# An encoder trunk's instruction planner: two DMA queues that share the rings, a margin behind each landing, and rotary queries written as whole rows

## The chip, the core and the metric

One core of a Trainium2 chip runs the whole program as one launch. TensorE (PE) multiplies, and its weight loads (PEld) overlap the multiplications; VectorE (DVE) and ScalarE (ACT) do elementwise work; GpSimd (POOL) and SyncE (SP) issue DMAs here and compute next to nothing. The metric is the device time of one execution in microseconds (us), as a median of several.

## The reference, cut to what matters

```python
for l in range(2):                                   # x: (1, 512, 1024) float32
    h = rmsnorm(x, g_mix[l])
    y_a = differential_attention(rope(h @ Wq), rope(h @ Wk), h @ Wv)   # 4 heads, two softmaxes each
    y_b = dilated_attention(...)                     # 3 (window, dilation) groups, 4 heads each
    c_q, c_kv = rmsnorm(h @ Wcq), rmsnorm(h @ Wckv)  # MLA: 768 and 256 wide
    qh = (c_q @ w_uq).reshape(S, 8, 64 + 32)         # 8 heads: 64 plain and 32 rotary columns
    q = concat(qh[..., :64], rope(qh[..., 64:]))     # the rotary part is the one rewritten
    y_c = softmax(q @ k.T * 96 ** -0.5) @ v
    x = x + (sum(sigmoid(gate_i) * y_i) ) @ w_out[l]
    x = x + square(relu(rmsnorm(x, g_mlp[l]) @ w_up[l])) @ w_down[l]
return rmsnorm(x, g_final)
```

## The kernel before, in words

Activations lie transposed: 128 features on the partitions, 512 tokens along the row. Every product is taken in three passes of float32r: weights and activations are split into a high and a low half, and `mm3` issues high x high, high x low and low x high. So each block of weights goes through the same steps: a DMA into a buffer `raw`, an ACT copy `w<-raw` (high half), a DVE subtraction `w<-raw,w` (low half), and then some 24 matmuls of 512 columns. Most weight loads are issued by POOL; those of the rotary query/key units (`qk_unit`, labels du0 to du3, bs0, bs1, bo00 to bo11) and of `w_uq` (labels rq and mq0 to mq3) are issued by SP, together with all small transfers.

The engines' work is first recorded and then planned. `trunk` calls engine objects whose methods only append an `Op` to a `Plan`; `record` finds its predecessors and `cost` its assumed duration. `Plan.schedule` then plays the program through, event by event: each engine takes, of its operations that are ready, the one with the lowest key, if its buffers can be had (42 slots of 1024 words, at most 6 of them `raw`). `emit` writes the operations out in the order of their planned starts, one order over all engines. On the chip only each engine's own order and the semaphores count; the planned times exist nowhere. An engine takes its instructions strictly in that order, so an ACT copy whose load is late holds back every ACT instruction behind it.

Of a DMA the plan assumes a transfer time `lat` on the 16 engines and an extra time `more`; one number `pipe` says when the transfers entered so far are through, whichever queue issued them. When a DMA is finished in the plan, its readers on compute engines become ready `dslack` (100 ns) later:

```python
if op.eng in dmaq and ops[s].eng not in dmaq:
    f += o["dslack"]
```

The program of a layer: `ckv` and `cq` (MLA inputs), `KV`, then `run` interleaves attention steps (label A) with projections in the order of `SEQS`, then `wout`, then `mlp`. Of the names in the rows: `s` are score banks, `p` the softmax numerators, `tp`/`pt` transposed ones, `av` attention outputs, `mm` projection banks, `x` here the MLP's product banks, `rx` rotated queries and keys, `dq`, `dk`, `kdr`, `krd`, `rqd` DRAM scratch through which they are regrouped, `qk` the regrouped ones, `al` and `ml` small bounces of the dilated groups, `fs` that of a row sum. `mla_rotary` computes all 8 heads' rotary queries at once (its 128 rows are 8 heads of 16 pairs), writes both halves to `rqd`, and `mla_q` reads each head's part back. All engine instructions stem from one line of `emit` (L565), so the profile's rows are told apart by tile names.

Of the kernel before, what the change touches and what calls it, by code (L numbers as in the profile page):

```python
# [20 lines left out]
S = 512  # L21
# [79 lines left out]
class Plan:  # L101
# [142 lines left out]
    def cost(self, eng, m, args, kw, reads, writes):  # L244

        def free(v):
            n = 1
            for d in (v.shape if isinstance(v, View) else v.shape)[1:]:
                n *= d
            return n  # L250
        o = args[0]
        if "dma" in m:
            def run(v):
                r = 1
                for st, k in reversed((v.ap if isinstance(v, View) else v).ap):
                    if st != r:
                        break
                    r *= k
                return r
            src = args[1]  # L260
            size = 4 * free(o) * o.shape[0]
            b = 4 * min(run(o), run(src))
            k = size / b

            per = next((c for w, c in ((64, 9), (128, 15), (256, 22), (512, 31), (1024, 65)) if b <= w), 112 * b / 2048)
            lat = k * per / 16
            out = not isinstance(o, View) or o.buf.space == "D"
            rows = min([bin(r[0]).count("1") for r in (self.region(v) for v in (o, src) if isinstance(v, View)
                                              and v.buf.space == "S")])
            self.more = 1100 if out else 2000  # L270
            if b > 64 and rows >= 16:
                self.more += 1.2 * lat * (128 / rows - 1)
            if out and b <= 8:
                self.more += k * (16 if b == 4 else 8)
            if not (isinstance(src, View) and src.buf.space == "S") and any(
                    st == 0 for st, _ in (src.ap if isinstance(src, View) else src).ap):
                self.more += 2200
            return 900 if eng == "gpsimd" else 475 if k <= 256 else 600, lat
        n = free(o)
        psum = any(isinstance(v, View) and v.buf.space == "P" for v in reads)  # L280
        if m == "transpose":
            return 109, 200
        if m == "matmul":
            r = args[2]
            f = free(r)
            if r.ap.dtype == F32:
                if self.label == "warm":
                    return 8 * f / 2.4, 200
                return 214 if f == 1 else 4 * f / 2.4, 200
            return max(109, 0.4415 * f + 5), 200  # L290
        if eng == "scalar":
            d = n / 1.2 + (52 if psum else 94)
            if isinstance(kw.get("scale"), View) or isinstance(kw.get("bias"), View):
                d += 93
            if kw.get("accum_out") is not None:
                d += 93
            return d, 155
        if m == "reduce_max":
            n = free(args[1])
        if m == "tensor_scalar" and n > 64 and not psum:  # L300
            return n / 1.92 + 130, 130
        if m == "tensor_scalar" and psum and n > 8:
            return n / 0.96 + 125, 130
        if m == "scalar_tensor_tensor" and isinstance(args[2], View):
            return n / 0.96 + 130, 130
        return n / 0.96 + 69, 130


    def schedule(self):
# [53 lines left out]
                heapq.heappush(pend[op.eng], (ready[op.i], op.i))  # L363
        frees = []
        dmaq = ("gpsimd", "sync")
        pipe = 0.0
        inq = 0.0
        entry = []
        t = 0.0
# [46 lines left out]
        def finish(op, fin):  # L416
# [6 lines left out]
            for s in op.succ:  # L423
# [9 lines left out]
                if not npred[s]:  # L433
                    heapq.heappush(pend[ops[s].eng], (ready[s], s))

        def bank_free(op):

            return max((x for b in op.bufs if b.space == "P" for e, x in b.last.items() if e != op.eng), default=0.0)

        while nleft:  # L440
            while entry and entry[0][0] <= t:
                te, _, op = heapq.heappop(entry)
                inq -= op.lat
                pipe = max(pipe, te) + op.lat
                finish(op, pipe + op.more + o["dmalat"])
            while frees and frees[0][0] <= t:
                release(heapq.heappop(frees)[-1])
            progress = False
            for e in engs:
                pe_, av_ = pend[e], avail[e]  # L450
                while pe_ and pe_[0][0] <= t:
                    i = heapq.heappop(pe_)[1]
                    heapq.heappush(av_, (ops[i].key, i))
                if free_t[e] > t or not av_ or e == "gpsimd" and max(pipe, t) + inq - t > o["backlog"]:
                    continue
                skipped = []
                pick = None
                while av_ and len(skipped) < 40:
                    c = heapq.heappop(av_)
                    w = bank_free(ops[c[1]])  # L460
                    if w > t:
                        heapq.heappush(pe_, (w, c[1]))
                        continue
                    if try_alloc(ops[c[1]]):
                        pick = ops[c[1]]
                        break
                    skipped.append(c)
                for c in skipped:
                    heapq.heappush(av_, c)
                if pick is None:  # L470
                    continue
                op = pick
                progress = True
                op.start = t
                free_t[e] = t + op.dur
                done[op.i] = True
                nleft -= 1
                while frontier < N and done[frontier]:
                    frontier += 1
                for b in op.bufs:  # L480
                    if b.users[-1] is op and b.words > 8 and b.cls:
                        u = [x for x in b.users if not done[x.i]]
                        if u:

                            b.users = sorted([x for x in b.users if done[x.i]], key=lambda x: x.i) + u
                            rel[u[-1].i].append(b)
                            if u[-1].i not in alloc_seen(evs, u[-1].i):
                                bisect.insort(evs, u[-1].i)
                if e in dmaq:
                    inq += op.lat  # L490
                    heapq.heappush(entry, (t + op.dur + o["entry"], op.i, op))
                else:
                    if e == "tensor":
                        tensor_busy += op.dur
                    fin = t + op.dur + op.lat
                    for b in op.bufs:
                        if b.space == "P":
                            b.last[e] = fin
                    finish(op, fin)
# [9 lines left out]
                nt.append(frees[0][0])  # L509
            if entry:  # L510
                nt.append(entry[0][0])
            if avail["gpsimd"]:
                nt.append(max(pipe, t) + inq - o["backlog"] + 1)
            nt = [x for x in nt if x > t]
            if not nt:
                f = ops[frontier]
# [2 lines left out]
            t = min(nt)  # L519
        while entry:  # L520
            te, _, op = heapq.heappop(entry)
            pipe = max(pipe, te) + op.lat
            op.end = pipe + op.more + o["dmalat"]
        self.makespan = max(op.end for op in ops)
        self.busy = tensor_busy

# [52 lines left out]
def trunk(ctx, tc, x, w_in, b_gate, g_mix, diff_lambda, g_diff, g_cq, g_ckv, w_uq, w_ukv,  # L579
# [4 lines left out]
    sb = ctx.enter_context(tc.tile_pool(name="sb", bufs=1))  # L584
    ps = ctx.enter_context(tc.tile_pool(name="ps", bufs=1, space=PSUM))
    dr = ctx.enter_context(tc.tile_pool(name="dr", bufs=1, space=DRAM))
    opts = dict(n2=12, n4=42, limits=dict(x0=8, mm=5, s=3, tp=2, av=2, raw=6, w=12, p=8, pd=4, pt=4), boost=20, vecs=14e3, warm=6, backlog=6000, slack=150, late=120, dmalat=-750, dslack=100, entry=300, begin=dict(gpsimd=1075, sync=560), lifo=1, ahead=dict(xt=300, raw=350, tb=300))
    plan = Plan(nc, sb, ps, x, {8: 64, 512: opts["n2"], 1024: opts["n4"]}, opts)
    ten, act, dve = plan.tensor, plan.scalar, plan.vector

# [19 lines left out]
    def dma(dst, src):  # L610
        return plan.sync.dma_start(dst, src)
# [217 lines left out]
    def layer(l, norm):  # L829
# [178 lines left out]
                dve.tensor_sub(V[b][:, :, lo:lo + 64], src[:, :, hd], V[b][:, :, hi:hi + 64])  # L1008

        wq4 = w_uq[l].rearrange("(k p) (h d) -> p k h d", p=128, d=96)  # L1010
        rqd = plan.dram(dr.tile([8, 2, 16, 2, S], F32, name=f"rqd{l}"))

        def rope(x1, x2, c, s, near=False):

# [14 lines left out]
        def mla_rotary():  # L1029
# [14 lines left out]
                mm3(p, wh, wl, cq)  # L1044
                xp.append(p)
            r1, r2 = rope(xp[0], xp[1], mrq[0], mrq[1])
            dma(rqd[:, 0], r1.bitcast(F32))
            dma(rqd[:, 1], r2.bitcast(F32))

        def mla_q(pr):  # L1050
            rw = T("raw")[:, :768].rearrange("p (k h d) -> p k h d", h=2, d=64)
# [9 lines left out]
            for i in range(2):  # L1061
                hd = 2 * pr + i
                qq, kk = H("qk"), H("qk")
                dma(qq.bitcast(F32)[0:64], t.bitcast(F32)[64 * i:64 * i + 64])
                dma(qq.bitcast(F32)[64:96], rqd[hd].rearrange("a d b n -> (a d) b n"))
                dma(kk.bitcast(F32)[0:64], kdr[pr][i])
                dma(kk.bitcast(F32)[64:96], krd)
                heads.append((qq, kk))
# [757 lines left out]
```

## Time and profile before

| what | value |
|---|---|
| median of 3 runs | 1974.43 us (1973.69 to 1976.33) |
| the profiled execution's own time | 1968.35 us |
| its span, first to last instruction | 1966.6 us |
| PE busy | 1917.2 us (97%) |
| DVE, ACT busy | 1425.8 us (73%), 943.4 us (48%) |
| granted TensorE clock, mean | 0.993 |

The table's busy times are of the profiled execution. PE's 97% says that PE has little idle time to give back; a time is gained only where PE waits.

### The profile page before, as it was taken

How to read it: one execution, taken by the hardware profiler on the slowest of the kernel's cores; microseconds unless marked ns; L12 is line 12 of the kernel's file. 1: busy time of each engine (PE TensorE's matmuls, PEld its weight loads, DVE VectorE, ACT ScalarE, POOL GpSimd, SP SyncE). 2: the span in 40 equal slices, each digit the busy share in tenths (PEclk: the TensorE clock that was granted, in tenths of full speed). 3: DMA queues.
4: the chain of work that ended last, by engine and by line, in shares of the span. 5: the costliest groups of instructions: out<-in, count | busy, mean ns of one | idle time of the engine just before them, and what ended most of it. 6: DMA issues, size and time to landing. Idle time of an engine off the chain costs nothing.

```text
span 1966.6 us, 28095 instructions
## 1 busy us (share of the span) xinstructions
PE 1917.2 (97%) x10468; PEld 1637.1 (83%) x10468; DVE 1425.8 (73%) x3017; ACT 943.4 (48%) x1739; POOL 213.6 (11%) x260
## 2 busy tenths in 40 slices
PE   8999999999999999999999998999999999999998
PEld 7788778887878898898887877888877888998987
DVE  6688867778866656778557976687888766666874
ACT  5465544545444554544344744455444345545442
POOL 1000001000111020111100000001002110111200
PEclk9999999999999999999999999999999999999999
DMA  7944626567654242335347364456666442333431
GB/s 223 201 116 128 202 70 190 171 153 209 189 166 127 76 129 65 108 86 171 117 105 190 84 192 119 129 149 182 163 199 189 144 135 66 111 87 106 142 95 44
DMA packets 193537, 271.72 MB, mean 138 GB/s; under 512 B 98220, under 2 KB 128940, under 8 KB 193400
## 3 DMA queue, kind: packets, MB, share of 16 engines
q1 hardware_dynamic: 157080, 137.53, 25.6%
q0 software_dynamic: 36320, 132.40, 22.9%
q8 instruction: 82, 1.34, 0.3%
q14 instruction: 55, 0.45, 0.1%
HBM read 215.02 MB, written 50.67 MB: 135 GB/s over the span
## 4 chain that ended last, share of the span: by engine, by line
PE 78%; DMA 9%; DVE 8%; issue 3%; ACT 1%; SPq 1%; DVEq 0%; ACTq 0%; POOLq 0%
PE mm L565 56%; PE x L565 12%; PE s L565 4%; PE av L565 3%; DMA raw<-in_w_in_dram 3%; PE tp L565 3%; DVE w L565 2%; DVE t L565 1%; DVE sm L565 1%; DMA sm<-al 1%; SPq L565 1%; DMA al<-sm 1%; DMA raw<-in_w_uq_dram 1%; DVE oo L565 1%; DVE rx L565 1%
## 5 line engine op out<-in xcount | busy, mean ns | idle before, releaser
L565 PE MATMUL mm<-h,w 128*128 128x512 f32 x3936 | 968.7, 397 | 0.0
L565 PEld LDWEIGHTS mm<-h,w 128*128 128x128 f32 x3936 | 729.9, 189 | 159.9 <-issue 0.6
L565 DVE TENSOR_TENSOR w<-raw,w 128x1024 fp32r<-128x1024 f32 (+3 forms) x390 | 362.7, 945 | 74.0 <-ACT w L565 63.0
L565 ACT ACTIVATE w<-raw 128x1024 fp32r<-128x1024 f32 (+3 forms) x390 | 314.8, 831 | 170.0 <-DMA raw<-in_w_in_dram 57.2
L565 PEld LDWEIGHTS x<-u,w 128*128 128x128 f32 x2016 | 239.5, 189 | 1.0 <-DVE u L565 0.5
L565 PE MATMUL x<-u,w 128*128 128x256 f32 x2016 | 239.9, 281 | 0.3 <-DVE u L565 0.3
L565 POOL DMA_DIRECT2D raw<-in_w_in_dram x86 | 74.8, 871 | 848.2 <-PE mm L565 301.6
L565 PE MATMUL mm<-w,h 128*128 128x256 f32 (+1 forms) x1152 | 155.5, 286 | 0.0
L565 PEld LDWEIGHTS mm<-w,h 128*128 128x128 f32 x1152 | 149.4, 190 | 3.6 <-DVE w L565 0.4
L565 PE MATMUL s<-qk,qk 96*128 96x512 f32 (+2 forms) x448 | 128.3, 372 | 7.1 <-DVE sm L565 4.2
L565 PE MATMUL mm<-co,w 128*128 128x512 f32 x456 | 117.1, 402 | 4.5 <-ACT w L565 4.1
L565 ACT ACTIVATE p<-s,sm 128x512 f32<-128x512 f32 x128 | 87.2, 685 | 62.6 <-DVE sm L565 62.2
L565 ACT ACTIVATE t<-mm 128x512 f32<-128x512 f32 x74 | 44.3, 598 | 144.9 <-PE mm L565 144.8
L565 ACT ACTIVATE pt<-tp 128x512 fp32r<-128x512 f32 x128 | 71.7, 595 | 86.7 <-PE tp L565 84.3
L565 DVE TENSOR_TENSOR t<-mm,const 128x512 f32<-128x512 f32 (+1 forms) x98 | 64.3, 675 | 58.3 <-PE mm L565 57.9
L565 PEld LDWEIGHTS mm<-co,w 128*128 128x128 f32 x456 | 85.0, 191 | 23.9 <-ACT w L565 4.5
L565 PE MATMUL av<-pt,v 128*128 128x256 f32 x576 | 97.2, 291 | 4.6 <-ACT pt L565 2.8
L565 PE MATMUL mm<-om,w 128*128 128x512 f32 x384 | 100.3, 396 | 0.0
L565 DVE TENSOR_REDUCE sm<-s 128x1 f32<-128x512 f32 x128 | 86.2, 683 | 19.3 <-PE s L565 18.9
L565 PEld LDWEIGHTS s<-qk,qk 128*128 128x128 f32 (+1 forms) x448 | 81.8, 193 | 22.0 <-DVE sm L565 5.6
L565 PEld LDWEIGHTS av<-pt,v 128*128 128x128 f32 x576 | 82.3, 189 | 20.7 <-ACT pt L565 8.5
L565 PE MATMUL mm<-u,w 128*128 128x512 f32 (+1 forms) x432 | 89.9, 369 | 0.0
(166 smaller groups left out, 2205.2 us busy)
## 6 DMA issues: line engine op xcount, KB each, us to landing
raw<-in_w_in_dram POOLq DMA_DIRECT2D x80, 512.0 KB, 6.3
raw<-in_w_up_dram POOLq DMA_DIRECT2D x64, 512.0 KB, 4.9
raw<-in_w_down_dram POOLq DMA_DIRECT2D x64, 512.0 KB, 5.0
dk<-rx SPq DMA_DIRECT2D x40, 512.0 KB, 4.5
qk<-dk SPq DMA_DIRECT2D x40, 512.0 KB, 6.9
raw<-in_w_in_dram SPq DMA_DIRECT2D x24, 512.0 KB, 7.1
dq<-rx SPq DMA_DIRECT2D x40, 256.0 KB, 4.4
qk<-dq SPq DMA_DIRECT2D x20, 512.0 KB, 4.5
```

The lines of the kernel that those rows point to most:

```text
L565: getattr(getattr(self.nc, op.eng), op.m)(*args, **kw)
```

## The change

`Plan.schedule` no longer keeps one `pipe`. Each queue (POOL's and SP's) has a list `flow` of transfers in order, the heads of both lists proceed at once at half speed each, and a queue alone has full speed. The margin `dslack` goes from 100 to 2000 ns. `cost` gets other extra times for transfers with runs of 4, 8 and 16 bytes. And the scratch `rqd` is laid out as two blocks of 128 whole rows: each half is written as one 128-row transfer in place of 8 x 16 rows, and a head's 32 rotary rows are read by two DMAs of 16 rows in place of one of 32. No arithmetic of the network changes.

```diff
-            if out and b <= 8:
-                self.more += k * (16 if b == 4 else 8)
+            if out and b <= 16:
+                self.more += k * {4: 16, 8: 5, 16: 3}[b]
+            if not out and b == 8:
+                self.more += 2000
...
-        pipe = 0.0
+        flow = {e: [] for e in dmaq}
+        flow_t = 0.0
...
+        def flow_next():
+            n = sum(1 for q in flow.values() if q)
+            return min((flow_t + n * q[0][0] for q in flow.values() if q), default=None)
+
+        def flow_to(x):
+            nonlocal flow_t
+            while True:
+                nx = flow_next()
+                n = sum(1 for q in flow.values() if q)
+                if nx is None or nx > x + 1e-6:
+                    for q in flow.values():
+                        if q:
+                            q[0][0] -= (x - flow_t) / n
+                    flow_t = x
+                    return
+                for q in flow.values():
+                    if q:
+                        q[0][0] -= (nx - flow_t) / n
+                flow_t = nx
+                for q in flow.values():
+                    if q and q[0][0] <= 1e-6:
+                        op = q.pop(0)[1]
+                        finish(op, nx + op.more + o["dmalat"])
+
+        def flow_left():
+            return sum(x[0] for q in flow.values() for x in q) + inq
...
-                pipe = max(pipe, te) + op.lat
-                finish(op, pipe + op.more + o["dmalat"])
+                flow[op.eng].append([op.lat, op])
+            flow_to(t)
...
-                if free_t[e] > t or not av_ or e == "gpsimd" and max(pipe, t) + inq - t > o["backlog"]:
+                if free_t[e] > t or not av_ or e == "gpsimd" and flow_left() > o["backlog"]:
...
-    opts = dict(n2=12, n4=42, limits=dict(x0=8, mm=5, s=3, tp=2, av=2, raw=6, w=12, p=8, pd=4, pt=4), boost=20, vecs=14e3, warm=6, backlog=6000, slack=150, late=120, dmalat=-750, dslack=100, entry=300, begin=dict(gpsimd=1075, sync=560), lifo=1, ahead=dict(xt=300, raw=350, tb=300))
+    opts = dict(n2=12, n4=42, limits=dict(x0=8, mm=5, s=3, tp=2, av=2, raw=6, w=12, p=8, pd=4, pt=4), boost=20, vecs=14e3, warm=6, backlog=6000, slack=150, late=120, dmalat=-750, dslack=2000, entry=300, begin=dict(gpsimd=1075, sync=560), lifo=1, ahead=dict(xt=300, raw=350, tb=300))
...
-        rqd = plan.dram(dr.tile([8, 2, 16, 2, S], F32, name=f"rqd{l}"))
+        rqd = plan.dram(dr.tile([2, 128, 2, S], F32, name=f"rqd{l}"))
...
-            dma(rqd[:, 0], r1.bitcast(F32))
-            dma(rqd[:, 1], r2.bitcast(F32))
+            dma(rqd[0], r1.bitcast(F32))
+            dma(rqd[1], r2.bitcast(F32))
...
-                dma(qq.bitcast(F32)[64:96], rqd[hd].rearrange("a d b n -> (a d) b n"))
+                for a in range(2):
+                    dma(qq.bitcast(F32)[64 + 16 * a:80 + 16 * a], rqd[a, 16 * hd:16 * hd + 16])
```

Since every operation's place follows from the plan, the order differs on all engines. Three places show how.

ACT, first layer, at the first weight block of unit du2. Before (`raw_2673` is du2's first load, issued by SP):

```order
206 L565 ACTIVATE th_2655<-th_2655,const_477 128x512
207 L565 ACTIVATE o_2669<-av_2639 128x256
208 L565 ACTIVATE p_2688,sm_2689<-s_2667,sm_2680 128x512
209 L565 ACTIVATE p_2704,sm_2705<-s_2685,sm_2696 128x512
210 L565 ACTIVATE w_2732<-raw_2673 128x8x64
211 L565 ACTIVATE w_2738<-raw_2673 128x8x64
212 L565 ACTIVATE th_2742<-th_2742,const_477 128x512
213 L565 ACTIVATE p_2756,sm_2757<-s_2715,sm_2729 128x512
214 L565 ACTIVATE w_2765<-raw_2671 128x1024
215 L565 ACTIVATE p_2774,sm_2775<-s_2727,sm_2748 128x512
216 L565 ACTIVATE w_2732<-raw_2678 128x8x64
217 L565 ACTIVATE w_2738<-raw_2678 128x8x64
```

The same place in the change, where that load is `raw_2683`:

```order
205 L600 ACTIVATE rx_2672<-t_2629 128x512
206 L600 ACTIVATE o_2679<-av_2644 128x256
207 L600 ACTIVATE th_2669<-th_2669,const_456 128x512
208 L600 ACTIVATE p_2697,sm_2698<-s_2652,sm_2676 128x512
209 L600 ACTIVATE p_2710,sm_2711<-s_2691,sm_2701 128x512
210 L600 ACTIVATE th_2740<-th_2740,const_456 128x512
211 L600 ACTIVATE p_2752,sm_2753<-s_2719,sm_2729 128x512
212 L600 ACTIVATE p_2759,sm_2760<-s_2727,sm_2746 128x512
213 L600 ACTIVATE w_2775<-raw_2681 128x1024
214 L600 ACTIVATE w_2786<-raw_2683 128x8x64
215 L600 ACTIVATE pt_2792<-tp_2734 128x512
216 L600 ACTIVATE pt_2796<-tp_2738 128x512
```

The copy of du2's block now stands behind one `th` and two softmax steps `p` that stood behind it before.

SP, first layer, at the rotary queries. Before (`rx_1095`, `rx_1099` are the two rotated halves):

```order
58 L565 DMA rqd_80<-rx_1095 8x16x1024
59 L565 DMA rqd_80<-rx_1099 8x16x1024
60 L565 DMA qk_1124<-rx_1113 64x1024
61 L565 DMA qk_1130<-rx_1113 64x1024
62 L565 DMA qk_1158<-rx_1147 64x1024
63 L565 DMA qk_1164<-rx_1147 64x1024
64 L565 DMA qk_1124<-rqd_80 32x1024
65 L565 DMA qk_1130<-rqd_80 32x1024
66 L565 DMA qk_1158<-rqd_80 32x1024
67 L565 DMA qk_1164<-rqd_80 32x1024
```

And in the change:

```order
58 L600 DMA rqd_80<-rx_1095 128x1024
59 L600 DMA rqd_80<-rx_1099 128x1024
60 L600 DMA qk_1122<-rx_1113 64x1024
61 L600 DMA qk_1126<-rx_1113 64x1024
62 L600 DMA qk_1159<-rx_1145 64x1024
63 L600 DMA qk_1165<-rx_1145 64x1024
64 L600 DMA qk_1122<-rqd_80 16x1024 x2
65 L600 DMA qk_1126<-rqd_80 16x1024 x2
66 L600 DMA qk_1159<-rqd_80 16x1024 x2
67 L600 DMA qk_1165<-rqd_80 16x1024 x2
```

The writes have 128 rows in place of 8 x 16, and each read stands as two of 16 rows. SP issues 16 DMAs more over both layers.

DVE, first layer, at the low halves of the weight block bv1 (the loads are `raw_3767` and `raw_3776`). Before:

```order
612 L565 SCALAR_TENSOR_TENSOR v_3827<-mm_3824,const_596,v_3827 128x64 x2
613 L565 SCALAR_TENSOR_TENSOR v_3836<-mm_3824,const_596,v_3836 128x64 x2
614 L565 TENSOR_TENSOR w_3897<-raw_3767,w_3879 128x4x128
615 L565 TENSOR_TENSOR w_3904<-raw_3767,w_3887 128x4x128
616 L565 TENSOR_TENSOR w_3897<-raw_3776,w_3879 128x4x128
617 L565 SCALAR_TENSOR_TENSOR v_3827<-mm_3865,const_596,v_3827 128x64
618 L565 TENSOR_TENSOR sm_3930<-sm_3891,sm_3706 128x4
619 L565 SCALAR_TENSOR_TENSOR v_3827<-mm_3865,const_596,v_3827 128x64
620 L565 TENSOR_SCALAR sm_3930<-sm_3930 128x4
621 L565 SCALAR_TENSOR_TENSOR v_3836<-mm_3865,const_596,v_3836 128x64
622 L565 TENSOR_SCALAR sm_3940<-sm_3930 128x4
623 L565 SCALAR_TENSOR_TENSOR v_3836<-mm_3865,const_596,v_3836 128x64
```

In the change the loads are `raw_3772` and `raw_3811`, the first one's low halves stand just ahead of these rows, and those of the second are rows 619 and 625:

```order
614 L600 TENSOR_TENSOR w_3937<-raw_3753,w_3918 128x8x64
615 L600 TENSOR_TENSOR w_3943<-raw_3753,w_3928 128x8x64
616 L600 TENSOR_REDUCE sm_3951<-s_3935 128x1
617 L600 TENSOR_REDUCE sm_3957<-s_3949 128x1
618 L600 TENSOR_SCALAR sm_3951<-sm_3951 128x1
619 L600 TENSOR_TENSOR w_3893<-raw_3811,w_3877 128x4x128
620 L600 TENSOR_SCALAR sm_3957<-sm_3957 128x1
621 L600 SCALAR_TENSOR_TENSOR v_3831<-mm_3904,const_599,v_3831 128x64 x2
622 L600 RECIPROCAL const_3983<-sm_3974 128x1
623 L600 SCALAR_TENSOR_TENSOR v_3838<-mm_3904,const_599,v_3838 128x64
624 L600 TENSOR_TENSOR sm_3991<-sm_3921,sm_3690 128x4
625 L600 TENSOR_TENSOR w_3900<-raw_3811,w_3885 128x4x128
```

Three of the four low halves stood one behind the other; the second load's are now behind score reductions and value splits of later work.

## Rows read from the trace of the kernel before

**Rows 1.** The page's head: span, and busy time of each engine.
```profile
span 1966.6 us, 28095 instructions
...
PE 1917.2 (97%) x10468; PEld 1637.1 (83%) x10468; DVE 1425.8 (73%) x3017; ACT 943.4 (48%) x1739; POOL 213.6 (11%) x260
```

**Rows 2.** Waits of PE: who waited for whom; us in total, times, longest.
```profile
PE tp L565 <- DVE p L565: 12.3, 5, 5.8
PE s L565 <- DVE sm L565: 4.2, 2, 2.1
PE mm L565 <- ACT w L565: 4.1, 1, 4.1
PE x L565 <- DMA v<-in_x_dram: 3.9, 2, 2.3
PE tp L565 <- DVE sm L565: 3.6, 3, 1.8
PE tp L565 <- DVE pd L565: 3.5, 4, 1.7
PE s L565 <- DMA qk<-rqd: 2.9, 1, 2.9
PE av L565 <- ACT pt L565: 2.8, 3, 1.3
...
PE x L565 <- DVE u L565: 0.3, 1, 0.3
```

**Rows 3.** The chain, stretch 1195 to 1220: start, us, what.
```profile
1199.07 11.08 DMA raw<-in_w_in_dram
...
1210.17 0.03 ACT w L565
...
1216.72 0.76 DVE p L565
```

**Rows 4.** PE's timeline at three waits; idle time before, and its end, in brackets.
```profile
97.63 0.72 PE L565 MATMUL mm<-co,w 128*128 128x512 f32 x2 [4.08 <-ACT w L565]
...
248.26 0.44 PE L565 MATMUL tp<-const,p 128*128 128x128 f32 x2 [4.30 <-DVE p L565]
...
1217.52 0.69 PE L565 MATMUL tp<-const,p 128*128 128x128 f32 x2 [5.81 <-DVE p L565]
```

**Rows 5.** The chain over the whole span, longest pieces.
```profile
70.88 4.20 DMA kdr<-rx
...
82.61 14.03 DMA raw<-in_w_uq_dram
...
230.76 10.12 DMA raw<-in_w_in_dram
...
684.58 39.61 PE x L565 x336
724.19 44.63 PE mm L565 x192
...
1055.97 8.96 DMA rqd<-rx
...
1352.54 6.78 DMA raw<-in_w_in_dram
```

**Rows 6.** Waits of ACT and DVE on DMAs; us in total, times, longest.
```profile
ACT w L565 <- DMA raw<-in_w_in_dram: 57.2, 23, 7.9
...
DVE pd L565 <- DMA sm<-al: 16.8, 8, 4.1
```

**Rows 7.** Stages 1055 to 1065: engines busy, PE clock, DMA share, GB/s.
```profile
1055.00:1060.00 5.00, 5.00 (x23) 4.06 (x22) 3.77 (x5) 2.91 (x4) 0.00 (x0) 1.00 0.38 75
1060.00:1065.00 5.00, 5.00 (x30) 4.28 (x28) 1.29 (x2) 0.79 (x2) 0.00 (x0) 1.00 0.79 230
```

**Rows 8.** Instructions on tiles rqd and dk: ns min/median/max; landing times in us.
```profile
L565 SPq DMA_DIRECT2D qk<-rqd x16: 336/443/1613, 101.6 to 1070.1; - x16
...
DMA to landing us min/median/max: 4.5/5.0/9.3
```

More of the change, by code (lines that the diff above doesn't have):

```diff
@@ L442, in schedule @@
                 te, _, op = heapq.heappop(entry)
+                flow_to(te)
                 inq -= op.lat
-                pipe = max(pipe, te) + op.lat
-                finish(op, pipe + op.more + o["dmalat"])
+                flow[op.eng].append([op.lat, op])
+            flow_to(t)
             while frees and frees[0][0] <= t:
@@ L511, in schedule @@
                 nt.append(entry[0][0])
-            if avail["gpsimd"]:
-                nt.append(max(pipe, t) + inq - o["backlog"] + 1)
+            nx = flow_next()
+            if nx is not None:
+                nt.append(nx)
+            if avail["gpsimd"] and flow_left() > o["backlog"] and flow_left() > inq:
+                nt.append(t + flow_left() - o["backlog"] + 1)
             nt = [x for x in nt if x > t]
@@ L521, in schedule @@
             te, _, op = heapq.heappop(entry)
-            pipe = max(pipe, te) + op.lat
-            op.end = pipe + op.more + o["dmalat"]
+            flow_to(te)
+            flow[op.eng].append([op.lat, op])
+        flow_to(flow_t + 1e6)
         self.makespan = max(op.end for op in ops)
```

## The prediction

> **What bounds the kernel now.** The page first: PE is busy for 1917.2 of 1966.6 us [rows 1], so at most 49.4 us are idle, and no shorter list of matmuls is offered by this change. Next the waits of PE [rows 2], which tell what the idle time is made of: its eight largest rows are 37.3 us. 3.9 of them are the first loads of x, which no order of the program removes; 33.4 us are waits inside the program, nearly all of them on softmax pieces (`tp<-p`, `av<-pt`, `s`) that DVE and ACT deliver late. So PE is bound by its own work plus some thirty microseconds in which ACT and DVE are late.
>
> Why they are late is read from the chain around the largest of these waits [rows 3]. PE waits 5.81 us at 1217.52 for a softmax numerator [rows 4], that comes from a DVE step at 1216.72, and following it back the chain leads to an ACT copy `w<-raw` at 1210.17 and to a load of `w_in` that took 11.08 us. ACT takes its instructions in order: the copy for unit du2 stands ahead of the softmax exponentials, its data is not there, and the exponentials that PE needs stand behind it. The first layer's twin waits 4.30 us at 248.26 [rows 4] behind a load of 10.12 us [rows 5]; at 97.63 PE waits 4.08 us for the split of `w_uq` weights whose load took 14.03 us [rows 4, 5]. ACT's waits show how general this is: 23 waits on loads of `w_in`, 57.2 us, and on DVE 8 waits, 16.8 us, on the alpha bounce `sm<-al` [rows 6]. The waits of PE that I followed back have this one cause: a reader stands in its engine's order earlier than its DMA lands.
>
> **The margin and the two queues.** They add and remove no instruction; they move readers back. I measured the move in matmuls. The program is written out in one order over all engines, so between a DMA's place and the place of its first reader a number of matmuls stand; a matmul of 512 columns costs 44.63 / 192 = 0.232 us and one of 256 columns 39.61 / 336 = 0.118 us [rows 5]. I call that sum the lead of a load. Where the landing takes longer than the lead, the reader blocks its engine. By this count:
>
> - du2's first load, both layers: lead 5.5 before, 9.7 in the change; landing 10.12 and 11.08 [rows 3, 5]. The ACT rows in the change's section show it: the copy went behind `th`, `p`, `p`. What is left is 0.4 + 1.4 = 1.8 us.
> - the second `w_uq` load of mq2: lead 7.9 to 12.4, landing 14.03 [rows 5]; 1.6 us is left.
> - the last load of bo01: lead 8.6 to 11.3, landing 6.78 [rows 5]; its reader waited because SP had issued the load late. Nothing is left.
> - the alpha bounces: four reads per layer, leads 3.3, 5.8, 2.5 and 3.7 to 5.1, 8.0, 4.6 and 4.4 in the first layer, 1.7 more on average; DVE's mean wait is 16.8 / 8 = 2.1 [rows 6], so 0.4 is left of each. Two scores waits of 2.1 (`s<-sm`) and the `tp<-pd` waits of 3.5 in all [rows 2] are these. For the rest I take 1.0 us.
> - first rotary read of the second layer: PE waits 2.9 for it [rows 2]; between the write and the score matmul 9.2 us of matmuls stood, now 11.3. By the lead alone 0.8 is left.
>
> The leads of other loads grow alike: of 296 loads whose landing the trace has, 39 took longer to land than their lead before, 14 than their lead in the change, and where they are still short it is mostly by 1 to 2 us or at the start. Left in all: 1.8 + 1.6 + 1.0 + 0.8 = 5.2 us; removed 33.4 - 5.2 = **28.2 us**. Bounds: nothing, if landings move with the leads (a rival), and all 33.4.
>
> **The rotary rows.** Before, the write of both halves lands 8.96 us after its issue, where a write of the same 512 KB by rows of all partitions, `kdr<-rx`, took 4.20 [rows 5]. In 1055 to 1060, in which it runs, the DMA engines are busy for 0.38 of the time at 75 GB/s, and then 0.79 at 230 [rows 7]: the rings are not full while it is written. So its cost in the change lies between 4.20 and 8.96. I take 8.96, that is no gain, because what is left of this wait is 0.8 us and is counted above; with 4.20 these 0.8 go too. The Trainium skill has a rule for this, in "DMA: Bandwidth & Descriptors", section "Why a DMA increments its semaphore by 16 and not by 1": a DMA runs on as many engines, at most 16, as divide the slowest dimension of both sides, so a leading 8 gives 8 engines and 128 rows give 16. The half-idle rings of [rows 7] agree; by that rule the write halves and the sum gains the 0.8.
>
> The reads cost more: 16 issues of 0.443 us [rows 8], 7.1 us of SP. SP does nothing else than issue and wait, so only the issues ahead of the first head of each layer are on the path: 2 x 0.443 = **0.9 us** added. Uncovered, all 7.1 would be. The same page's "Rules for kernel authors" speaks against the edit: two transfers to disjoint halves of the partitions share the same engines, so one is to be preferred. No row here shows a pair of halves; by that rule the pair moves as fast as the whole did, and the sum keeps the 0.9.
>
> **What the margin costs.** A later split stands nearer to its matmuls. Counted in the same way from a low half on DVE to the first matmul that reads it, 7 of 318 splits stood closer than 2 us before and 19 do in the change; the median falls from 19.5 to 16.6. The new ones are in dv0 and mq2 of the first layer and, in both layers, in du1, y26, bv0, bv1 and bo00; the DVE rows show bv1, whose second load's low halves went behind score reductions and value splits. A late neighbour on DVE or ACT now reaches PE there. Below the price is nothing: among PE's waits on splits [rows 2] there is a single one of size, 4.1, it is the late load of mq2, and none is at the seven near ones. Above it is that 4.1 each, 49 us for twelve. I take 0.5 each, near to the seven: **6 us**. Two thirds of all splits keep over 10 us, which hides the rest.
>
> **The regrouped keys of du1.** Their reads `qk<-dk` now stand 6.0 us of matmuls ahead of their scores, 14.1 before; the longest landing of such a read is 9.3 [rows 8], measured at this unit, beside du2's loads that shared the rings. In the change SP issues du2's loads ahead of them. Between 0 and 2 x 3.3 us; I take half, **3.3 us**.
>
> The start (PE's first loads), the MLP and the other prices of short runs I cost at nothing: the MLP's products wait 0.3 us in all [rows 2], as their weights are split well ahead, and without that cover each of its blocks would wait as bv1 may; at the start the landing of x decides, at most its 3.9 us [rows 2] either way.
>
> **The sum.** 28.2 removed, 0.9 + 6 + 3.3 = 10.2 added: 18.0 us less. The profiled execution took 1968.35 us in all (span 1966.6 and 1.75 around it), so 1950.4; the median of the runs shown is 6.1 above that execution, so **1956 us**.
>
> **Rivals.**
> 1. More is gained: the splits near their matmuls cost nothing, du1's keys land in time, the rotary wait goes: 33.4 less, 1941. For it: the seven near splits that cost nothing. Against: ACT and DVE rows are busy for 48% and 73% [rows 1], and small waits move along.
> 2. SP becomes the late one: 16 more issues (7.1) and du1's keys (6.6) all reach PE; with the 6 of the splits 28.2 - 19.7 = 8.5 less, 1966. For it: an issue can take 1.613 us instead of 0.443 [rows 8]. Against: PE waited only 2.9 us directly on what SP fetches last, the rotary rows [rows 2].
> 3. Slower: the twelve new near splits, first of all bv1 and bo00, where four loads land together. Each is now behind softmax work that itself waits for PE, so a delay runs in a circle. It decides from (28.2 - 4.2) / 12 = 2.0 us each; at the 4.1 of [rows 2] it is 49 + 4.2 - 28.2 = 25 more, 1999; at 3 us each 1986. Against it: medians of 16.6 us elsewhere.
> 4. The change doesn't do what it says: the leads grow, but the loads land later by as much, as the buffers and rings they wait for are freed by the same moved readers. Then the waits stay, 1974. For it: a lead is a distance in the order and says nothing on when SP can issue. Against: the loads of 10.12 and 11.08 us take long though they are issued in time, and where SP issued one late (bo01) the landing was 6.78 [rows 3, 5].
>
> **How the numbers follow.** Forecast 0.60 (own range 1946 to 1967), rival 1 0.10, rival 2 0.10, rival 3 0.12, rival 4 0.08. The range of 1940 to 1973 takes in the forecast and rivals 1 and 2, 0.80. A measurement of this kernel tells a change from none at about 0.2%, 4 us. Faster than 1970.5: 0.60 + 0.10 and most of rival 2, 0.78. Within: the rest of it and most of rival 4, 0.09. Slower: rival 3 and a rest, 0.13.
>
> **What the changed kernel's profile would show.** If right: PE's waits on `tp<-p` fall from 12.3 to under 4 us and `mm<-w` does not grow beyond 6; the chain has no load of `w_in` of SP that is followed by an ACT copy, a DVE step and a PE wait; `rqd<-rx` lands in about 4 to 6 us; ACT's waits on `w_in` fall from 57.2 to under 20. The prediction is wrong if PE's waits on `w` rise by over 10 us, at bv1 and bo00 first, or if `s<-qk` waits for `dk` in both layers.

## The result, and the profile after

The changed kernel takes **1940.4 us** (median of 4 runs, 1936.89 to 1941.78), beside it the kernel before 1974.06 (1971.57 to 1976.33). The ratio is 0.9827, interval 0.9809 to 0.9845. 18 us less was forecast and the median is 33.7 less: the direction held, the size did not, and 1940.4 lies at the very lower end of the range of 1940 to 1973. The profiled execution of the change is 1941.78, its span 1940.0.

Its page shows what [rows 1] showed, and the chain by engine, which was 78% PE, 9% DMA and 8% DVE before:

```profile
span 1940.0 us, 28120 instructions
...
PE 1910.4 (98%) x10468; PEld 1634.1 (84%) x10468; DVE 1420.0 (73%) x3017; ACT 942.1 (49%) x1739; POOL 213.2 (11%) x260
...
PE 88%; DVE 4%; DMA 4%; issue 3%; ACT 1%; SPq 0%; DVEq 0%; ACTq 0%; POOLq 0%
```

The waits of PE, all of those listed in the trace of the change, against [rows 2]:

```profile
PE tp L600 <- DVE pd L600: 4.8, 4, 1.4
PE x L600 <- DMA v<-in_x_dram: 4.3, 2, 2.2
PE s L600 <- DVE sm L600: 4.3, 2, 2.2
PE mm L600 <- ACT h L600: 1.7, 1, 1.7
PE mm L600 <- DVE t L600: 1.5, 1, 1.5
PE av L600 <- DVE pt L600: 1.2, 4, 0.5
PE mm L600 <- ACT w L600: 1.0, 1, 1.0
PE mm L600 <- DVE sm L600: 1.0, 2, 0.5
PE mm L600 <- DVE w L600: 0.5, 1, 0.5
PE tp L600 <- DVE p L600: 0.5, 2, 0.3
PE tp L600 <- DVE sm L600: 0.2, 1, 0.2
```

They are 21.0 us in all, 41.3 before. The waits behind SP's loads are gone: `tp<-p` 12.3 to 0.5, `av<-ACT pt` 2.8 to nothing, `mm<-ACT w` 4.1 to 1.0, and `s<-qk<-rqd` 2.9 to nothing. Two are not gone: `s<-sm` has the same two waits of 2.2, and `tp<-pd` grew from 3.5 to 4.8. ACT's waits on `w_in` and the DMAs on `rqd`, against [rows 6] and [rows 8]; first the waits, then from the list of DMAs KB each and median us to landing:

```profile
ACT w L600 <- DMA raw<-in_w_in_dram: 31.6, 17, 5.5
```

```profile
rqd<-rx SPq DMA_DIRECT2D x4, 512.0 KB, 5.6
qk<-rqd SPq DMA_DIRECT2D x32, 64.0 KB, 2.6
```

The listed waits are 20.3 us less and the span is 26.6 less; the median is 33.7 less. PE's busy time fell too, from 1917.2 to 1910.4 us with the same count of matmuls, so it is not true that a time is gained only where PE waits. Most of what is missing is in a column that the prediction did not use, the granted clock of TensorE. Stretches of the trace of before around the rotary queries' wait of 2.9 us at 1068.15 in the second layer; the columns are length, busy time of PE, PEld, DVE, ACT, POOL, granted clock, DMA share, GB/s:

```profile
1066.00:1067.00 1.00, 0.00 (x0) 0.00 (x0) 0.00 (x0) 0.00 (x0) 0.00 (x0) 1.00 0.86 258
1067.00:1068.00 1.00, 0.00 (x0) 0.00 (x0) 0.00 (x0) 0.00 (x0) 0.00 (x0) 0.98 1.00 229
1068.00:1069.00 1.00, 0.84 (x2) 0.78 (x3) 0.00 (x0) 0.00 (x0) 0.00 (x0) 0.50 1.01 205
1069.00:1074.00 5.00, 5.00 (x17) 4.22 (x17) 2.88 (x8) 1.56 (x5) 0.00 (x0) 0.50 1.05 220
1074.00:1075.00 1.00, 1.00 (x6) 0.85 (x5) 0.65 (x2) 0.67 (x2) 0.00 (x0) 0.61 1.06 213
1075.00:1076.00 1.00, 1.00 (x6) 0.83 (x5) 0.60 (x1) 0.00 (x0) 0.00 (x0) 1.00 0.47 90
```

PE waits until 1068.15, and the clock that it then works at is 0.50, that is 1.2 in place of 2.4 GHz, until near 1075. PE is 100% busy there and does 17 matmuls in 5 us, in the last row 6 in 1 us. While PE is busy, 0.42 + 2.50 + 0.39 = 3.3 us of full-speed work are lost (busy time by the share of the clock that is missing), behind a wait of 2.9. No list of waits shows it, since PE is busy. In slices of 1 us, the trace of before has five such stretches inside the program (at 98, 248, 1067, 1166 and 1214). By the column they lose 1.7 or 3.4 us each, 11.9 in all; 1.5 of that lies in PE's own waits at 1067 and 1214, where nothing is lost, so 10.4 are lost beside the waits. Each stretch follows one of the waits that [rows 2] sums or begins in it. The trace of the change has four (at 8, 97, 476 and 1428), 8.5 by the column and 6.9 beside the waits. At the end of both there is one more in which PE has nothing left to do; it costs nothing. Of the 26.6 us, 20.3 are waits and 3.5 clock; 2.8 lie in pieces too small for these lists.

The same account for every kernel below: listed waits of PE plus the time lost by the clock inside the program while PE is busy. "Clock" is the median of the mean granted clocks of that kernel's runs.

| kernel | median us | ratio to before | clock | span of the profiled run | waits | lost by the clock | span less both |
|---|---|---|---|---|---|---|---|
| before | 1974.06 | 1 | 0.991 | 1966.6 | 41.3 | 10.4 | 1914.9 |
| the change | 1940.40 | 0.9827 | 0.9955 | 1940.0 | 21.0 | 6.9 | 1912.1 |
| e1_margin | 1949.41 | 0.9871 | 0.996 | 1947.6 | 27.8 | 3.7 | 1916.1 |
| e2_flow | 1964.6 | 0.9953 | 0.991 | 1955.5 | 33.0 | 6.5 | 1916.0 |
| e3_rows | 1962.98 | 0.9943 | 0.994 | 1966.6 | 39.1 | 8.8 | 1918.7 |
| e4_norows | 1942.52 | 0.9841 | 0.997 | 1941.9 | 21.0 | 3.4 | 1917.5 |
| e5_again | 1973.61 | 1.001 | 0.991 | 1968.5 | 41.7 | 10.4 | 1916.4 |
| e6_shift | 1966.18 | 0.9956 | 0.993 | 1963.6 | 38.3 | 11.9 | 1913.4 |
| e7_price | 1930.11 | 0.9781 | 0.9985 | 1929.2 | 16.1 | 3.4 | 1909.7 |
| e8_m4000 | 1931.23 | 0.9789 | 0.9985 | 1928.3 | 14.8 | 0 | 1913.5 |
| e9_unshift | 1949.73 | 0.9883 | 0.995 | 1950.1 | 27.4 | 8.2 | 1914.5 |
| e10_ctl150 | 1972.18 | 0.9999 | 0.991 | 1969.6 | 42.0 | 11.9 | 1915.7 |
| e11_ctl50 | 1972.16 | 0.9991 | 0.991 | 1971.9 | 40.2 | 17.1 | 1914.6 |
| e12_p4000 | 1936.0 | 0.9812 | 0.995 | 1937.4 | 19.9 | 6.3 | 1911.2 |

(The clock of before is that of 15 to 19 runs beside the experiments, whose medians were 1972.42 to 1973.33.) The spans lie 43.6 us apart, the last column 9.0. So waits and clock together carry most of the larger differences. The clock is also much of what differs from run to run. Before's fastest execution beside the experiments, 1967.99 us, and its slowest, 1985.83, are one program: among 53 executions of it, the two with a mean clock of 0.987 have a median of 1983.0 us, the 17 with 0.991 one of 1972.6, the three with 0.994 one of 1968.4. That is 14.7 us for 0.007 of the clock, where 0.007 of the span is 13.8.

### The profile page after: what moved, and what is told of

The parts are those of the page before. It is cut to its first block, busy times and chain, and to the rows that moved or that the text cites. A ratio compares the mean times of both kernels' runs of the same rounds, so it can differ in the third digit from the quotient of the medians.

```text
span 1940.0 us, 28120 instructions
## 1 busy us (share of the span) xinstructions
PE 1910.4 (98%) x10468; PEld 1634.1 (84%) x10468; DVE 1420.0 (73%) x3017; ACT 942.1 (49%) x1739; POOL 213.2 (11%) x260
## 4 chain that ended last, share of the span: by engine, by line
PE 88%; DVE 4%; DMA 4%; issue 3%; ACT 1%; SPq 0%; DVEq 0%; ACTq 0%; POOLq 0%
PE mm L600 65%; PE x L600 13%; PE s L600 4%; PE tp L600 3%; PE av L600 3%; DMA ml<-sm 1%; DVE sm L600 1%; DVE oo L600 1%; DMA sm<-ml 1%; DVE w L600 1%; DMA sm<-al 1%; DMA v<-in_x_dram 1%; DMA raw<-in_w_in_dram 1%; DVE pt L600 0%; DVE t L600 0%
## 5 line engine op out<-in xcount | busy, mean ns | idle before, releaser
L600 PE MATMUL s<-qk,qk 96*128 96x512 f32 (+2 forms) x448 | 122.5, 365 | 4.3 <-DVE sm L600 4.3
L600 DVE TENSOR_TENSOR pt<-tp,pt 128x512 fp32r<-128x512 f32 x128 | 84.1, 683 | 8.7 <-ACT pt L600 8.1
```

What stands on the lines that cost most here:

```text
L600: getattr(getattr(self.nc, op.eng), op.m)(*args, **kw)
```

## The experiments

**e1_margin.** The kernel before with the margin alone.

```diff
-dslack=100,
+dslack=2000,
```

> The kernel before with the margin of 2000 ns alone (one pipe, old prices, old rotary scratch). Theory A (readers moved behind their landings are what pays, and the margin does it): the leads of du2's first load grow from 5.6 to 10.0 us and of mq2's second from 7.9 to 9.3, loads with a lead under their landing fall from 39 to 8; PE's waits on softmax pieces mostly go, du2's 4.3 and 5.8 to under 1 each, mq2's 4.1 stays in good part; 18 to 26 us less than before. Rival B (the forecast of two queues does it, the margin adds little): under 8 us less.

24 us less than the kernel before beside it (1973.33), ratio 0.9871 (0.985 to 0.9891): the larger part of the change is this one number. Its largest waits:

```profile
PE mm L565 <- ACT w L565: 6.4, 2, 6.0
PE x L565 <- DMA v<-in_x_dram: 4.2, 2, 2.8
PE s L565 <- DVE sm L565: 4.1, 2, 2.1
PE tp L565 <- DVE pd L565: 3.7, 4, 1.6
```

`tp<-p` is down to 0.5 and the late `w_uq` load of mq2 stays, even with 6.0 in place of 4.1. ACT waits only 12.4 us for `w_in` here, less than half of the change's 31.6, and the kernel is yet 9 us slower: ACT's waits on loads were no measure of what reaches PE.

**e2_flow.** The change with the old margin and the old scratch, so that the two queues and the prices of short runs are left.

```diff
-dslack=2000,
+dslack=100,
...
-        rqd = plan.dram(dr.tile([2, 128, 2, S], F32, name=f"rqd{l}"))
+        rqd = plan.dram(dr.tile([8, 2, 16, 2, S], F32, name=f"rqd{l}"))
...
```

> The change without the margin (100 ns) and without the new rotary scratch: the two queues and the prices of short runs alone. Theory A: the leads of mq2, du1 and du2 grow here too (du2 5.6 to 11.9, du1 7.3 to 11.2, mq2 7.9 to 11.1), so their waits of PE go, about 16 us; but short leads of POOL's loads stay many (46 of 296), so ACT still waits on loads and 8 to 18 us less in all. Rival B: nearly the whole 34 us. Rival C (neither alone): within 4 us of before.

8.7 us less, ratio 0.9953 (0.9935 to 0.9971). `tp<-p` falls to 1.9, but `tp<-sm` grows to 6.2 and `av<-pt` to 5.8: the two queues move the readers of SP's loads, and with so small a margin other pieces take their place. Its profiled execution is the fastest of its ten, at a clock of 0.996 where their median is 0.991; so its row in the table shows less time lost by the clock than its usual run has.

**e3_rows.** The kernel before with the new layout of `rqd` alone.

```diff
-        rqd = plan.dram(dr.tile([8, 2, 16, 2, S], F32, name=f"rqd{l}"))
+        rqd = plan.dram(dr.tile([2, 128, 2, S], F32, name=f"rqd{l}"))
...
```

> The kernel before with the new rotary scratch alone. Theory A: leads as before; the wait of PE of 2.9 us for the first rotary read of the second layer goes or shrinks, so 0 to 3 us less, not told from no change. Rival D (16 more DMAs on SP and the halves cost): up to 7 us more. The write, 8.96 us to its landing before, lands in 4 to 6 us if the rings were half idle because of its shape.

10.4 us less, ratio 0.9943 (0.9921 to 0.9964), where nothing to 3 was expected. Of the second layer's two writes, one for each half, the first lands in 2.67 us where it took 7.11 before, and the second in 3.34 where it took 8.96 [rows 5] (for the writes that the lists give no landing, from the last update of their semaphore in the trace). PE no longer waits for them, and the same place of the program, some 4 us later in this trace (the first of these scores at 1072.40 in place of 1068.15), keeps its clock:

```profile
1066.00:1076.00 10.00, 10.00 (x56) 8.59 (x55) 4.28 (x10) 2.42 (x5) 0.00 (x0) 1.00 0.84 205
```

So the edit gives back the wait of 2.9 and the 3.3 behind it, 6.2 us. In all six profiled executions that have the old scratch and a margin of 50 to 150 (before, e2, e5, e6, e10, e11) the clock falls at this place and some 3 us are lost. The medians of the clocks, 0.991 and 0.994, are worth 5.9 us of the 10.4, the wait 2.9; 1.6 are left, which is little beside the width of the interval (7 to 15 us). The profiled execution of this kernel was the slowest of its six runs and has no gain at all (span 1966.6 as before): the wait is gone, but the stretch of slow clock at 97 is twice as long, one at 490 is new, and 3.8 us more lie in pieces below the lists (last column). So the 10 us are shown by the medians; how they are made up is in part argued. From that one trace the edit would have been called useless.

**e4_norows.** The change with the old scratch: e3's diff the other way.

> The change with the old rotary scratch. Theory A: like the change within 3 us, as its leads are the same and the first head stands 2 us later anyway. Rival D (the whole rows bring a part): 3 us or more above the change.

1942.52, 2 us above the change, which four runs of each don't tell from nothing: ratios 0.9841 (0.9816 to 0.9865) and 0.9827. The second write takes 9.41 us here, much as before, but the margin has moved the first head's scores so far behind it that PE waits 0.9 us at most, and the clock does not fall. So the same edit is worth 10 us alone and about 2, not told from nothing, behind the margin: e1, e2 and e3 sum to 43 us, and the change has 33.7.

**e5_again.** The kernel before, unchanged.

> The kernel before once more, unchanged, for a second trace and the spread of its executions. If its late loads are what makes its executions differ (theory A), the waits of PE on softmax pieces behind SP's loads differ from trace to trace by some us and its runs spread over 8 us or more, where those of the change spread over 5; if they don't (rival: a constant offset of profiled executions), this profiled execution lies some 5 to 6 us under its median again with the same waits.

1973.61, ratio 1.001 (0.9995 to 1.0026). Its waits are 41.7 beside 41.3 in all, and `s<-qk<-rqd` is again 2.9; small waits differ from place to place. Neither expectation holds as it was put: its ten runs spread over 7.6 us, and its profiled execution lies 3.3 under their median.

**e6_shift.** The kernel before; only the 16 weight splits of du2 stand 4.2 us later in the written order.

```diff
+    moved = [op for op in plan.ops if op.label == "du2" and op.args[0].buf.tag == "w" and op.eng in ("scalar", "vector")]
+    for op in moved:
+        op.start += 4200
```

> The kernel before, with one thing moved after planning: the 16 instructions that split du2's weights (both layers) are written out 4.2 us of planned time later, so that their lead is 9.8 in place of 5.6; every other instruction keeps its order. Theory A: PE's waits of 4.3 and 5.8 us fall to under 0.5 and 1.6, and 8 to 10 us come off. Rival (the load lands later by as much, or the softmax step waits elsewhere): under 3 us.

6.2 us less, ratio 0.9956 (0.9939 to 0.9973). PE's timeline at the two places, where [rows 4] had 4.30 and 5.81:

```profile
247.81 0.88 PE L565 MATMUL tp<-const,p 128*128 128x128 f32 x6 [2.02 <-DVE p L565]
...
1215.30 0.88 PE L565 MATMUL tp<-const,p 128*128 128x128 f32 x6 [1.61 <-DVE p L565]
```

6.5 us of the 10.1 are gone, so the copy behind the late load was what held PE; 8 to 10 us were expected. What holds it for 2 us more in the first layer is, by the chain, the next late load in the same way, which ACT's next copy waits for:

```profile
232.67 9.93 DMA raw<-in_w_o_mla_dram
...
242.63 1.07 ACT w L565
...
247.10 0.67 DVE p L565
```

**e9_unshift.** The converse: the change, with du2's splits 4.2 us earlier.

```diff
+        op.start -= 4200
```

> The change, with only du2's 16 weight splits written out 4.2 us earlier, the converse of e6_shift; all else stays in the change's order. Theory A (late readers of SP's loads block ACT, and that is most of what the margin removed): the two waits at du2 come back with 2 to 4 us each, some 5 to 8 us slower than the change, 1945 to 1949. Rival: the change owes its time to the new order as a whole, its other leads cover this one; less than 2 us slower.

1949.73, 9.3 above the change. Both waits are back, as PE's timeline shows:

```profile
241.66 0.69 PE L600 MATMUL tp<-const,p 128*128 128x128 f32 x2 [3.92 <-DVE p L600]
...
1200.54 0.69 PE L600 MATMUL tp<-const,p 128*128 128x128 f32 x2 [4.36 <-DVE p L600]
```

The chain in front of the first of them is again load, copy, softmax step:

```profile
227.95 9.17 DMA raw<-in_w_in_dram
...
237.14 0.63 ACT w L600
...
240.85 0.76 DVE p L600
```

The two waits are 8.3 us, and behind both the clock falls for some 3.4 us (1.7 each by the column). With e6 this shows the cause from both sides, and 16 instructions, eight in each layer, are worth 6.2 and 9.3 us beside the change's 33.7.

**e10_ctl150 and e11_ctl50.** The kernel before with a margin of 150 and of 50, two controls: the whole plan is made anew for a cause worth 0.6 us.

```diff
-dslack=100,
+dslack=150,
```

> The kernel before with a margin of 150 in place of 100 and nothing else: a control, planned anew with a cause that is worth 50/1900 of e1_margin's 24 us, 0.6 us. Theory A (what counts is how many readers stand before their landing): within 3 us of the kernel before. Rival C (any new plan draws its small waits anew, by 5 to 10 us either way, and e3_rows' 10 us are such a draw): 5 us or more away from the kernel before, in either direction.

> The kernel before with a margin of 50 in place of 100: the second control. Theory A: within 3 us of the kernel before. Rival C (a new plan is a new draw): 5 us or more away from it, in either direction; with e10_ctl150 the two give the size of that draw.

0.9999 (0.9982 to 1.0016) and 0.9991 (0.9976 to 1.0005). The orders did change: 264 and 233 of DVE's 3017 instructions stand in another place than in the kernel before, 200 in e3. A new plan is no draw of its own here; rival C falls, and e3's 10 us are not of that kind.

**e7_price.** The change, with the right price for one operation. In 455 to 475, ahead of the `s<-sm` wait at 474.76, DVE is busy for 18.78 of 20 us, and the additions `oo<-oo,av` of 64 x 256, which the plan prices at 336 ns, take 402/601/640 ns (min/median/max):

```profile
455.00:475.00 20.00, 17.84 (x97) 14.97 (x96) 18.78 (x37) 8.66 (x14) 2.40 (x3) 1.00 0.99 289
```

```profile
L600 DVE TENSOR_TENSOR oo<-oo,av x80: 402/601/640, 412.0 to 1514.1; 64x256 f32<-64x256 f32 x80
```

```diff
+        if m == "tensor_add" and len(o.shape) == 4:
+            return n / 0.96 + 350, 130
```

> The change, with one price more in the plan: DVE additions on views of four dimensions (the strided output additions of the dilated group, 0.62 us in the trace, 0.34 in the plan) are planned 0.28 us longer. Theory: the wait of 2.2 us per layer of PE's scores on DVE (s<-sm), that neither the margin nor the queues touch, is a backlog of DVE that the plan does not know of; it falls under 1, and 2 to 6 us come off the change, 1935 to 1938. Rival (DVE is simply full there): no change.

1930.11, 10.3 below the change, ratio 0.9781 (0.9755 to 0.9808). The `s<-sm` waits are gone and `tp<-pd` is 3.7. The largest rows:

```profile
PE x L602 <- DMA v<-in_x_dram: 4.5, 2, 2.8
PE tp L602 <- DVE pd L602: 3.7, 3, 1.9
PE mm L602 <- ACT h L602: 1.6, 1, 1.6
```

DVE's timeline in that stretch of the change agrees. The only idle pieces listed, one in front of the stretch and one within, are for PE and none for a DMA; the ten additions in it take 5.4 us, 2.0 more than planned, and the wait is 2.16:

```profile
455.15 1.29 DVE L600 TENSOR_TENSOR t<-mm,const 128x512 f32<-128x512 f32 x2 [3.21 <-PE mm L600]
...
465.08 0.69 DVE L600 TENSOR_TENSOR th<-mm,const 128x512 f32<-128x512 f32 x1 [0.50 <-PE mm L600]
```

So these two waits are made not by a late DMA, but by a DVE that the plan believed to be further on. The other row of this kind is another matter: two of the change's four `tp<-pd` waits, 1.27 and 1.16, still stand behind the alpha bounce. The chain at the first of them:

```profile
547.09 6.34 DMA sm<-al
...
553.46 0.36 DVE pd L600
...
553.87 0.82 PE tp L600 x4
```

That it is 10 us and not the expected few goes with what was found above: the waits are 4.9 us less, the change's clock fell behind each of the two waits (476, 1428), and the medians of the clocks, 0.9955 and 0.9985, are worth 5.8 us.

**e8_m4000.** The change with a margin of 4000 (`dslack=4000`).

> The change with a margin of 4000 ns. Theory A with a price of near splits: short leads fall from 14 to 5, splits nearer than 2 us grow from 19 to 22; little late loading is left to win, so within 4 us of the change. Rival E (a margin costs by itself, some 0.5 us at each near split): 3 us or more above it.

1931.23, 9.2 below the change, ratio 0.9789 (0.9762 to 0.9815), much more than expected. `s<-sm` and `tp<-pd` are gone here too, without a new price. That softmax pieces now stand ahead of the splits, which come later, may be the reason; it was not followed. Its largest wait inside the program:

```profile
PE mm L600 <- ACT w L600: 4.3, 3, 1.6
```

No stretch of slow clock is left in it before PE's last matmul.

**e12_p4000.** Both edits together.

> The change with both e7_price's row for strided additions and e8_m4000's margin of 4000. If the two remove different waits, they add up: 1940 - 10 - 9 = 1921. If they remove the same ones (both took away the score waits behind DVE), no more than the better alone: 1927 to 1931. Rival: with later splits and DVE work that is planned longer, weights come too near to their matmuls and waits on w grow: over 1933.

1936.0 (1932.62 to 1939.18), above either alone: they do not add up, and the rival's mechanism appears. PE's largest row of waits is now on low halves of weights, in each layer one, and behind both the clock falls (the first is shown). A `tp<-pd` wait of 3.0 at 540.98, with a longer fall of the clock, is as large:

```profile
PE mm L602 <- DVE w L602: 5.3, 2, 2.7
```

```profile
518.00:519.00 1.00, 0.00 (x0) 0.00 (x0) 1.00 (x1) 1.00 (x2) 0.00 (x0) 1.00 1.03 395
519.00:523.00 4.00, 3.81 (x10) 3.00 (x11) 2.40 (x3) 0.15 (x1) 2.49 (x3) 0.57 1.04 323
```

The fastest kernels are thus e7 and e8, some 2.1% below the kernel before, 9 to 10 us below the change; their intervals overlap.

## Why the prediction was off

**The cause was right for the part that it was read from.** Readers ahead of their landings blocked ACT, and PE waited for exponentials behind them: e6 and e9 show it for du2 from both sides, and e1 that the margin as a whole is worth 24 us. Rival 4 (landings move along) falls with `tp<-p` at 0.5. A part of it did happen: the median landing of SP's 512 KB loads of `w_in` went from 7.1 to 9.0 us; du2's first load in the first layer landed in 9.02, 10.12 before.

**The step that failed first is the size of a wait.** The prediction counted a wait with its listed length. It took the work behind a wait to run at full speed, without a reason. Here five of the waits, of 1.78 to 5.81 us, are followed by TensorE work at 1.2 GHz: at 98, 248, 1067, 1166 and 1214 in the kernel before, 10.4 us beside the 33.4 that were counted. The page prints the clock in tenths and shows a 9 in every slice; the table in front has a mean of 0.993. 0.007 of 1966.6 us is 13.8 us (2.2 of them behind PE's last matmul), a number that stood there to be read. The upper bound of what could be removed, all 33.4, was too low for the same reason: 33.7 came off with 10.8 us of those waits still there.

**The same step hid in the offset.** The median was forecast as the profiled time plus 6.1, as if that were a constant. It is mostly clock: the profiled execution of before had 0.993, the median of its runs 0.991, worth 3.9 us. The profiled execution of the change lies 1.4 above its median (0.995 beside 0.9955). Between the medians the clock gives 17.7 - 8.7 = 9.0 of the 33.7 us, an estimate from the mean clocks.

**Removed, term by term.** The seven rows that hold the 33.4 (without the start) are now 10.8, so 22.6 went where 28.2 were said.

- du2: nothing is listed where 1.8 was to stay. mq2: nothing beside 1.6; the 1.0 of `mm<-ACT w` stands at 94.91, at dv0 (`mm<-w,h`), whose load of `w_in` took 9.93. bo01: nothing, as said.
- the alpha bounces: 1.0 was to stay of `s<-sm` and `tp<-pd`, 9.1 stayed. DVE's own waits on the bounce did fall, from 16.8 to 3.2, but PE's did not follow: e7 shows that DVE's backlog made the `s<-sm` pair, and of `tp<-pd` 2.4 us are the bounce. The prediction had put both rows to the bounce as a whole and shows none of them followed back.
- the rotary rows: 0.8 stayed by the sum, nothing did. The price of the write of both halves was taken at 8.96; that is the second of the two writes alone. It takes 3.93 in the second layer of the change, below both ends of the bracket (the first 3.31, 7.11 before). In the first layer the two take 7.97 and 8.70, where other loads share the rings; 9.85 and 11.65 before. By the Trainium skill, "DMA: Bandwidth & Descriptors", section "Why a DMA increments its semaphore by 16 and not by 1", 128 rows use twice the engines of a leading 8. The traces agree: the semaphore of a write of 8 x 16 rows has one update some 1 us after its issue and eight more from 5.1 us on, that of a write of 128 rows sixteen. In the change's order this step mattered little (2 us, not told from nothing, e4); alone it is 10 (e3).

**Added, term by term.** The near splits were priced at 6 and show at most 2.5 us (at dv0, one of them, 1.0 and 0.5, and `mm<-sm` 1.0), du1's keys at 3.3 and show none, SP's 16 issues at 0.9 and show none: PE's list has no wait on `qk`. The warning in the Trainium skill, same page, "Rules for kernel authors", that two halves be one transfer, costs nothing here: a half lands in 2.6 us (median), a whole took 4.5. Rival 3 did not happen in the change, but e12 shows its mechanism at 2.7 us for one block in each layer, where a margin of 4000 and the longer DVE prices act together.

The smaller rows and the start grew by 2.3 in all. So 22.6 removed and 2.3 added (20.3) against 28.2 and 10.2 (18.0): two errors of 5.6 and 7.9 that nearly cancelled, by luck, and over them the clock, which was not in the sum. Rival 1 named 1941, but by a way that was not taken: all 33.4 us of waits gone, where 10.8 are left.

**What the profile was to show.** `tp<-p` under 4: 0.5. `mm<-w` not beyond 6: 1.5. No load of `w_in` by SP ahead of an ACT copy, a DVE step and a PE wait in the chain: none; the one that is left, in the first 100 us, was issued by POOL. `rqd<-rx` in 4 to 6: the 5.6 of the list is the median of 3.31 and 7.97, and none of the four writes lies in that range. ACT's waits on `w_in` under 20: 31.6, wrong, and e1 shows that the number says little of PE.

**What stays open.** The last column of the table still differs by 9.0 us, in pieces below what the lists show. Why a wait of 2.1 us at 1454.48 in the kernel before leaves the clock alone and one of 2.2 at 1426.99 in the change does not was not tested. What the 546.18 and 1498.06 waits of `tp<-pd` in the change wait for was not followed. How much of e2's gain is the two queues and how much the prices of short runs was not separated.

## What to carry to other kernels

Read the granted clock in short stretches behind each larger wait of PE and add what is lost there to the wait: here 10 us stood beside 33, and it is also much of what makes runs of one program differ. Before a class of waits is put down to one cause, follow one of each row back: of two rows of equal size here (4.1 and 4.2 us) one was a late DMA and one an engine whose work was underpriced in the plan. A margin wants a scan, and anew after each other change: 2000 and 4000 ns gave 1940 and 1931 us, and with longer DVE prices on top 4000 fell back to 1936.

## What was not expected of the hardware

- Some waits of 2.2 us and less are followed by TensorE at 1.2 GHz: after the wait of 2.16 us at 474.76 in the change the clock is 0.57 on average from 476 to 480, with PE busy all the time (12 matmuls in 4 us).

```profile
475.00:476.00 1.00, 1.00 (x6) 0.84 (x6) 0.97 (x2) 0.82 (x4) 0.00 (x0) 0.99 1.04 391
476.00:480.00 4.00, 4.00 (x12) 3.10 (x11) 1.75 (x6) 2.34 (x7) 0.00 (x0) 0.57 1.03 367
480.00:481.00 1.00, 1.00 (x6) 0.80 (x5) 0.61 (x1) 0.41 (x1) 0.00 (x0) 1.00 0.69 172
```

- Two writes of 512 KB, one behind the other, at the same place of the program (second layer): as 8 x 16 rows the first took 7.11 and 7.56 us and the second 8.96 and 9.41 (before, e4), as 128 whole rows 2.67 and 3.31, and 3.34 and 3.93 (e3, the change).
- An addition of 64 x 256 on DVE takes from 402 to 640 ns with the same count of elements. The output of the longer ones is strided in more dimensions; that this is the reason was not measured by itself.
